# Summing Strassen-Winograd products in one PSUM bank, and moving three modulations into the mixers' input products

## The chip, the cores and the metric

The kernel runs on one core of one Trainium2 chip. The metric is device time in microseconds (us) for one launch. The engines are named as in the profile: PE is TensorE (its weight loads are PEld), DVE is VectorE, ACT is ScalarE, POOL is GpSimd and SP is SyncE, which issues nearly all DMAs. PSUM has eight banks here: five under the name `ps`, two `pt`, one `po`, each of 128 x 512 fp32.

## The reference, cut to what matters

One diffusion-transformer layer on 1024 latent tokens and 256 context tokens, of width 1024, all fp32:

```
ml = split(silu(c) @ w_mod + b_mod, 9)              # nine modulations; mc likewise from c_ctx
x  = x + 0.5 * ml[2] * swiglu(modulate(rms_norm(x, norm1_g), ml[0], ml[1]), ffn1_w_in, ffn1_w_out)
...                                                  # cx likewise, with mc
hx = modulate(rms_norm(x, norm2_g), ml[3], ml[4])
bg, cg, vc, q, k, v, gt = split(hx @ w_in, ...)      # the input products of the mixers
y_conv = bg * short_conv(cg * vc, conv_w)
...                                                  # attention over context and latent keys: o
x  = x + ml[5] * (sigmoid(gt_c) * (y_conv @ w_branch_conv) + sigmoid(gt_a) * (o @ w_branch_attn)) @ w_out
x  = x + 0.5 * ml[8] * swiglu(modulate(rms_norm(x, norm3_g), ml[6], ml[7]), ffn2_w_in, ffn2_w_out)
return rms_norm(x, final_g)
# swiglu(h, w_in, w_out): a, b = split(h @ w_in, 2); (silu(a) * b) @ w_out
```

## The kernel before, in words

Activations lie transposed: channels on partitions, tokens along the free axis, in two chunks of 512 latent tokens, C0 and C1, and the context chunk CC. Each fp32 matmul is made of three: both operands are split into a high part (a cast by ACT) and the rest (a subtraction by DVE), and high*high, high*low and low*high are added in PSUM.

Three large products, the inputs of the two feed-forwards and those of the mixers, take their weights in *pairs of columns*: two blocks of 128 output channels (for a feed-forward, one of the half `a` and one of the half `b`). A pair's 2 x 2 blocks of weights times the 2 x 2 blocks of the activation (channel halves by token chunks) are computed by the Strassen-Winograd scheme with seven products instead of eight. Class `Winograd` holds it. Its seven right operands `r1` to `r7` are made once per stage; `lefts` makes the left operands pair by pair: two loads into `raw` (three buffers), three sums `s1`, `s2`, `s3` on POOL and a fourth that overwrites `s2`, and a split of each operand into a buffer `wl` (four buffers; ACT casts, then DVE subtracts). `product(i)` is one product: twelve matmuls of 512 columns into a fresh `ps` bank. There are 22 pairs in each feed-forward and 20 in the mixers.

The seven products of a pair are added up on DVE, each add reading one bank of PSUM: `first` copies product 1 to `u` (ACT) and adds 2 for `c`; `second` adds 6 to `u`, then 7 for `v`, and subtracts 4 from `v` for `b`; `third` adds 5 to `v` and to `u`, and 3 to `u`. The results are (c, b) for C0 and (u, v) for C1. `spill` takes silu(c) * b and writes it to DRAM (`hd`); in the mixers, conv and gates take their place.

In the first pairs of each stage (`ahead`: 13 in the first feed-forward, 9 in the mixers, 9 in the second) products 1 and 2, which need only C0's norm, run ahead of the others while C1's norm is made (`start`, `start_by_half`). Their `u` and `c` go to DRAM (`ucd`), all but the first two, and `fetch` brings them back one pair early. So an ahead pair has five products in the loop, in the order 6, 7, 4, 5, 3, and a later pair has seven, 1, 2, 6, 7, 4, 5, 3.

`later_mod(m)` computes a modulation: per half of 512 columns eight steps, each a load `rawm` and a multiply-add into `macc` on DVE, four empty steps, a split, six empty steps, two matmuls with `ones_r` and a DMA that turns the row into columns (`mcol`): 19 steps a half. Modulations 0 to 4 run in the first feed-forward. Modulation 5 (`mix_steps`, 8 steps in each round `i` of the mixers with `i > 2`), 6 and 7 (`late_steps`, while the branches are merged and `w_out` is applied) and 8 (`last_steps`, in the second feed-forward) come later. A round `i` of the mixers is two pairs, or three where `i` is odd.

From pair 14 on (`SIDE_FROM`) the first feed-forward also runs the context tokens with each pair's split weights (`side`), and after pair 13 it catches up on the first 14.

No order is written out by hand in these stages: a scheduler lists the instructions of each engine by a timeline of its own, and each engine then runs its list strictly in that order, waiting on semaphores. SP's DMA queue is such a list too.

Of the kernel before, what the change touches and what calls it, by code (L numbers as in the profile page):

```python
# [20 lines left out]
KD = D // P  # L21
# [19 lines left out]
SIDE_FROM = 14  # L41
# [10 lines left out]
def tile_dit_layer(  # L52
# [434 lines left out]
    class Winograd:  # L487
# [6 lines left out]
        def __init__(self, xs, gain, mod, m, pairs, plain=False, ahead=3, side_from=None):  # L494
# [10 lines left out]
            self.n_ahead, self.side, self.started, self.n_left = ahead, None, [], 0  # L505
# [46 lines left out]
        def norm1(self, turned=None):  # L552
# [23 lines left out]
            for k in range(4):  # L576
# [11 lines left out]
                dve.tensor_sub(out=t2, in0=t2, in1=f[:, 1])  # L588
# [24 lines left out]
        def lefts(self, pairs, side_from):  # L613
# [29 lines left out]
            for j, (wa, wb) in enumerate(pairs):  # L643
                side = side_from is not None and j >= side_from
                a, b = cols(wa), cols(wb)
# [4 lines left out]
                if j >= n:  # L650
                    yield from map(parts, a)
                yield parts(s2)
                yield parts(s3)
                if side:
                    yield parts(b[0])
                yield parts(b[1])
                yield parts(s1)
                pool.tensor_sub(out=s2, in0=a[1], in1=s2)
                yield parts(s2)
                if side_from is not None and j == side_from - 1:  # L660
                    for wa, wb in pairs[:side_from]:
                        yield from map(parts, cols(wa) + cols(wb))

# [12 lines left out]
        def terms(self, ps, w, i, k):  # L676
# [3 lines left out]
            matmul(ps, wh, r[:, 1], start=False, stop=False)  # L680
            matmul(ps, wl, r[:, 0], start=False, stop=k == 3)

        def product(self, i):
            w, ps = self.left(), ps_s()
            for k in range(4):
                self.terms(ps, w, i, k)
            if self.side:
                self.side(i, w)
            return ps

        def first(self):

            u, c = ttile("u"), ttile("c")
            act.copy(out=u, in_=self.product(1))
            dve.tensor_add(out=c, in0=u, in1=self.product(2))
            return u, c
# [61 lines left out]
        def next_first(self):  # L758
            if not self.started:
                return self.first()  # L760
            self.fetch()
            uc = self.started.pop(0)
            self.fetch()
            return uc

        def second(self, u):
# [1093 lines left out]
```

## Time and profile before

| | |
|---|---|
| three runs | 2680.39, 2682.8, 2686.76 us; median 2682.8 |
| the profiled execution | 2685.79 us, of which the span of the profile is 2684.0 |
| PE busy | 2639.7 us, 98% of the span |
| DVE busy | 2006.2 us, 75% |
| ACT busy | 1171.3 us, 44% |
| POOL busy | 557.9 us, 21% |
| DMA | 376.93 MB, mean 140 GB/s |
| mean granted PE clock | 0.995 |

The stages by their place in the span, read off the tiles in the trace: start and first norm to about 131 us, ahead pairs of the first feed-forward to about 309, pair 13 and the context's catching up to about 450, its later pairs to about 690, its output product to about 900; the mixers' start to about 950, their pairs to about 1290; keys, queries and attention to about 1835; merging and `w_out` to about 2021; the second feed-forward's start to about 2072, its pairs to about 2447, its output and the last norm to the end.

A PE that is busy is not necessarily at its peak: the ends of matmuls are modelled, so the number of matmuls in a stretch says as much as the busy time. The tables by stretches give, per engine, busy us and in brackets the number of instructions, then the granted clock as a share of full speed, the DMA engines' share and GB/s.

### The profile page before, as it was taken

The numbers are of one execution on the slowest core, as the hardware profiler recorded it, in microseconds if no ns is written. First come the engines' busy times: TensorE is split into PE (matmuls) and PEld (weight loads), VectorE is DVE, ScalarE is ACT, GpSimd is POOL, SyncE is SP. The second block draws the span as 40 slices with busy tenths as digits, with TensorE's granted clock in tenths as the row PEclk, the third lists the DMA queues.
The fourth block names the chain that finished last, engine by engine and source line by source line (L and its number), as shares of the span: only waits on it lengthen the run. The fifth ranks groups of instructions, "written<-read, shape, count | busy, mean of one in ns | idle before, by whom it ended". The sixth has DMA issues, their size and how long they took to land.

```text
span 2684.0 us, 36956 instructions
## 1 busy us (share of the span) xinstructions
PE 2639.7 (98%) x13373; PEld 2221.6 (83%) x13373; DVE 2006.2 (75%) x3356; ACT 1171.3 (44%) x2317; POOL 557.9 (21%) x449
## 2 busy tenths in 40 slices
PE   8999999999999999999999999999999999999998
PEld 5787899888778878888999888887888788888888
DVE  5788966888877899877387676675668876667885
ACT  6533454433444633333245566673236233334453
POOL 0134201211010044333032112141001442330200
PEclk9999999999999999999999999999999999999999
DMA  8565465345974345242312532113734543228741
GB/s 317 194 204 177 144 221 173 109 130 209 288 182 122 111 158 180 95 130 75 103 48 91 87 87 64 32 44 110 262 100 144 181 154 95 86 88 288 182 90 64
DMA packets 370000, 376.93 MB, mean 140 GB/s; under 512 B 19590, under 2 KB 258328, under 8 KB 369816
## 3 DMA queue, kind: packets, MB, share of 16 engines
q1 hardware_dynamic: 359000, 353.03, 40.8%
q0 software_dynamic: 10816, 21.53, 4.9%
q8 instruction: 105, 1.72, 0.3%
q14 instruction: 79, 0.65, 0.1%
HBM read 306.78 MB, written 67.67 MB: 140 GB/s over the span
## 4 chain that ended last, share of the span: by engine, by line
PE 84%; DVE 4%; DMA 2%; issue 2%; POOL 1%; ACT 1%; SPq 0%; DVEq 0%; POOLq 0%; ACTq 0%
PE ps L90 69%; PE pt L90 7%; PE po L90 7%; DVE wl L90 1%; DMA raw<-in_ffn_w_in_dram 1%; DMA ws<-in_ffn_w_out_dram 1%; DVE r L90 1%; DMA rawm<-in_w_mod_dram 1%; POOL s L90 0%; DVE macc L90 0%; POOL ol L90 0%; DVE u L90 0%; DVE uc L90 0%; DVE nt L90 0%; DVE v L90 0%
## 5 line engine op out<-in xcount | busy, mean ns | idle before, releaser
L90 PE MATMUL ps<-r,wl 128*128 128x512 f32 x5196 | 1204.7, 391 | 12.2 <-DVE wl L90 5.3
L90 PEld LDWEIGHTS ps<-r,wl 128*128 128x128 f32 x5196 | 971.6, 188 | 221.9 <-DVE wl L90 7.9
L90 ACT CAST wl<-s 128x512 fp32r<-128x512 f32 x254 | 156.7, 619 | 322.6 <-PE ps L90 219.3
L90 POOL TENSOR_TENSOR s<-raw 128x512 f32<-128x512 f32 x64 | 93.4, 1459 | 891.2 <-DMA raw<-in_ffn_w_in_dram 380.9
L90 ACT CAST wl<-raw 128x512 fp32r<-128x512 f32 x287 | 177.5, 619 | 219.6 <-PE ps L90 157.3
L90 DVE TENSOR_TENSOR wl<-raw,wl 128x512 fp32r<-128x512 f32 x287 | 201.9, 705 | 62.1 <-ACT wl L90 59.6
L90 DVE TENSOR_TENSOR wl<-s,wl 128x512 fp32r<-128x512 f32 x254 | 229.8, 905 | 21.3 <-ACT wl L90 19.7
L90 POOL TENSOR_TENSOR s<-raw,s 128x512 f32<-128x512 f32 x64 | 103.9, 1624 | 362.3 <-DVE wl L90 362.3
L90 DVE SCALAR_TENSOR_TENSOR macc<-rawm,silu_c,macc 128x512 f32<-128x512 f32 x178 | 149.8, 858 | 31.7 <-DMA rawm<-in_w_mod_dram 30.7
L90 PE MATMUL ps<-wh,r 128*128 128x256 f32 x768 | 141.6, 285 | 0.0
L90 DVE TENSOR_TENSOR u<-u,ps 128x512 f32<-128x512 f32 x174 | 118.0, 678 | 28.7 <-PE ps L90 28.5
L90 DVE TENSOR_TENSOR pts<-pt,pts 128x512 fp32r<-128x512 f32 x160 | 108.7, 685 | 35.7 <-ACT pts L90 33.5
L90 ACT CAST pts<-pt 128x512 fp32r<-128x512 f32 x160 | 93.3, 595 | 94.8 <-PE pt L90 90.9
L90 DVE TENSOR_REDUCE m<-ps 128x1 f32<-128x512 f32 (+1 forms) x192 | 109.9, 594 | 23.3 <-PE ps L90 22.3
L90 ACT CAST rh<-hid 128x512 fp32r<-128x512 f32 x132 | 80.9, 620 | 101.6 <-PE ps L90 89.3
L90 PE MATMUL ps<-rh,wl 128*128 128x512 f32 x360 | 122.3, 390 | 2.8 <-ACT rh L90 2.8
L90 PEld LDWEIGHTS ps<-wh,r 128*128 128x128 f32 x768 | 120.6, 192 | 0.0
L90 PE MATMUL po<-pts,vh 128*128 128x512 f32 x256 | 111.4, 440 | 0.2 <-ACT pts L90 0.2
L90 PE MATMUL ps<-wl,r 128*128 128x256 f32 x384 | 108.8, 283 | 0.0
L90 ACT CAST wh<-raw 128x512 fp32r<-128x512 f32 (+1 forms) x85 | 67.9, 801 | 88.8 <-PE ps L90 57.8
L90 DVE TENSOR_TENSOR rl<-hid,rh 128x512 fp32r<-128x512 f32 x132 | 89.8, 684 | 20.2 <-PE ps L90 9.8
L90 PE MATMUL ps<-kl,qs 128*128 128x512 f32 x384 | 104.3, 395 | 0.0
(314 smaller groups left out, 5118.6 us busy)
## 6 DMA issues: line engine op xcount, KB each, us to landing
raw<-in_ffn_w_in_dram SPq DMA_DIRECT2D x130, 512.0 KB
raw<-in_ffn_w_out_dram SPq DMA_DIRECT2D x72, 512.0 KB
rawm<-in_w_mod_dram SPq DMA_DIRECT2D x136, 256.0 KB
raw<-in_w_in_dram SPq DMA_DIRECT2D x61, 512.0 KB
hid<-hd SPq DMA_DIRECT2D x40, 512.0 KB
ws<-in_ffn_w_out_dram POOLq DMA_DIRECT2D x30, 512.0 KB, 6.6
ucd<-uc SPq DMA_DIRECT2D x25, 512.0 KB
hd<-c SPq DMA_DIRECT2D x40, 256.0 KB
```

The lines of the kernel that those rows point to most:

```text
L90: inst = getattr(self.engine, name)(*args, **kw)
```

## The change

The sums move from DVE into PSUM. Product 1 keeps its bank, called `x` here: 6 is added onto it, then 7, then the *negative* of 4 (its right operand is made with the sign turned, in `norm1`). Product 5 has a second bank, `z`, and 3 is added onto it. Between two products in the bank `x` ACT copies the partial sum out: after 1 (`u`, and `c` = `u` + product 2, as before), after 6 (`u6`) and after 7 (`v`). DVE adds `z` to `v` after product 5 and to `u6` after product 3; the results are (c, x) and (u6, v), where x is read from PSUM. For an ahead pair, ACT first copies the fetched `u` into the bank `x`. A pair's products are written in the order 6, 5, 7, then the next pair's head (its 6 if it is ahead, else its 1 and 2), then 4 and 3, then the next pair's 6 if it is not ahead; `order` gives the left operands in that order, and `fetch` loads a pair's weights when product 7 of the pair before asks for its operand.

Modulations 5, 6 and 7 all run in the mixers: 9 + 8 steps in each round from `i = 1`. None is left for merging and `w_out`. In the mixers a gate is written into a tile of its own.

```
@@ norm1
-                dve.tensor_sub(out=t2, in0=t2, in1=f[:, 1])
+                dve.tensor_sub(out=t2, in0=f[:, 1], in1=t2)
                 self.keep(4, k, t2)
@@ lefts
+            def fetch(j):
+                ...
+                a, b = map(cols, pairs[j])
+                s1, s2, s3 = ttile("s1"), ttile("s2"), ttile("s3")
+                pool.tensor_add(out=s1, in0=b[0], in1=b[1])
+                pool.tensor_sub(out=s2, in0=s1, in1=a[0])
+                pool.tensor_sub(out=s3, in0=a[0], in1=b[0])
+                state[j] = {0: b[0], 1: a[0], 2: a[1], 3: s2, 4: b[1], 5: s1, 6: s2, 7: s3}
+            for j, i in self.order(side_from):
+                ...
+                fetch(j)
+                yield parts(state[j][i])
+                if i == 6:
+                    pool.tensor_sub(out=state[j][3], in0=state[j][2], in1=state[j][3])
+                if i == 7 and j + 1 != side_from:
+                    fetch(j + 1)
@@ terms, product
-            matmul(ps, wh, r[:, 0], start=k == 0, stop=False)
+            matmul(ps, wh, r[:, 0], start=k == 0 and not on, stop=False, on=on)
...
-        def product(self, i):
-            w, ps = self.left(), ps_s()
+        def product(self, i, onto=None, j=None):
+            w, ps = self.left(), ps_s() if onto is None else onto
...
@@ first, second, third give way to
+        def head(self, j):
+            ...
+            if j < self.n_ahead:
+                self.fetch()
+                u, c = self.started.pop(0)
+                x = ps_s()
+                act.copy(out=x, in_=u)
+                self.fetch()
+                return x, self.with_sixth(x), c
+            u, c = ttile("u"), ttile("c")
+            x = self.product(1, j=j)
+            act.copy(out=u, in_=x)
+            dve.tensor_add(out=c, in0=u, in1=self.product(2, j=j))
+            return x, None, c
+        def with_sixth(self, x):
+            u = ttile("u6")
+            act.copy(out=u, in_=self.product(6, x))
+            return u
+        def results(self, apart=None):
+            opened = self.tail(self.head(0))
+            for j in range(self.n_pairs):
+                x, u, c = opened
+                z, v = self.product(5), ttile("v")
+                act.copy(out=v, in_=self.product(7, x))
+                dve.tensor_add(out=v, in0=v, in1=z)
+                ...
+                if j + 1 != apart:
+                    opened = self.head(j + 1)
+                self.product(4, x, j)
+                yield c, x
+                self.product(3, z)
+                dve.tensor_add(out=u, in0=u, in1=z)
+                if j + 1 != apart:
+                    opened = self.tail(opened)
+                yield u, v
+                ...
@@ modulations
-    mix_steps, late_steps, last_steps = later_mod(5), (step for m in (6, 7) for step in later_mod(m)), later_mod(8)
+    mix_steps, last_steps = (step for m in (5, 6, 7) for step in later_mod(m)), later_mod(8)
@@ mixers
-        if i > 2:
-            run(mix_steps, 8)
+        if i:
+            run(mix_steps, 9)
...
+        if i:
+            run(mix_steps, 8)
@@ merging, w_out
-                run(late_steps, 4)
...
-            if ch == C0:
-                run(late_steps, 4)
```

The lists of both programs hold the same number of matmuls on PE (13286). DVE's list has 256 instructions fewer, ACT's 159 more. Three places show how the lists change. In the rows, `ps`, `r` and `wl` carry a tile's running number, `r6` is the right operand of product 6, and `x3` at the end of a row stands for three matmuls in a row.

PE before, the mixers' first pair: products 6, 7, 4 and 5 each have a bank of their own.

```order
L90 MATMUL ps_1603_8818<-r6_1548_8592,wl_1584_8748 128x512 x3
L90 MATMUL ps_1603_8818<-r6_1563_8653,wl_1584_8748 128x512
L90 MATMUL ps_1605_8836<-r7_1512_8452,wl_1588_8768 128x512 x2
L90 MATMUL ps_1612_8863<-r4_1515_8462,wl_1590_8785 128x512 x2
L90 MATMUL ps_1603_8818<-r6_1563_8653,wl_1584_8748 128x512 x2
L90 MATMUL ps_1614_8880<-r5_1513_8455,wl_1602_8815 128x512 x2
```

PE after, the same place: the bank `ps_1525` is the bank `x` of this pair and `ps_1534` its bank `z`.

```order
L90 MATMUL ps_1525_8708<-r6_1488_8547,wl_1509_8642 128x512
L90 MATMUL ps_1534_8741<-r5_1487_8544,wl_1513_8663 128x512 x2
L90 MATMUL ps_1525_8708<-r6_1488_8547,wl_1509_8642 128x512 x2
L90 MATMUL ps_1525_8708<-r7_1437_8346,wl_1515_8680 128x512 x3
L90 MATMUL ps_1525_8708<-r7_1454_8413,wl_1515_8680 128x512 x3
L90 MATMUL ps_1525_8708<-r7_1471_8480,wl_1515_8680 128x512 x3
L90 MATMUL ps_1525_8708<-r7_1486_8541,wl_1515_8680 128x512 x3
L90 MATMUL ps_1537_8772<-r6_1439_8352,wl_1532_8721 128x512 x3
```

Product 7 now follows product 6 in the same bank with nothing between them, so that ACT's copy of `u6` lies between the two; the next pair's product 6 has moved up behind 7.

DVE before, the mixers' round `i = 3`, between the splits of products 2 (`wl_1797`) and 6 (`wl_1799`) of its last pair: `macc0` is a modulation's sum, `y` the short convolution.

```order
L90 TENSOR_TENSOR wl_1797_9847<-raw_1790_9820,wl_1797_9847 128x512
L90 SCALAR_TENSOR_TENSOR macc0_1775_9758<-rawm_1781_9774,silu_c_93,macc0_1775_9758 128x512
L90 TENSOR_TENSOR b_1785_9784<-v_1784_9783,ps_1796_9833 128x512
L90 SCALAR_TENSOR_TENSOR macc0_1775_9758<-rawm_1782_9777,silu_c_93,macc0_1775_9758 128x512
L90 TENSOR_SCALAR y_1801_9884<-u_1753_9642,cols_84 128x512
L90 TENSOR_TENSOR v_1784_9783<-v_1784_9783,ps_1798_9850 128x512
L90 TENSOR_TENSOR u_1754_9643<-u_1754_9643,ps_1798_9850 128x512
L90 TENSOR_TENSOR wl_1799_9865<-s2_1793_9825,wl_1799_9865 128x512
```

DVE after, the same round, from two rows behind the split of its first pair's product 7 to the split of the next pair's product 6 (`wl_1696`).

```order
L90 SCALAR_TENSOR_TENSOR macc0_1671_9472<-rawm_1674_9479,silu_c_93,macc0_1671_9472 128x512
L90 TENSOR_TENSOR v_1681_9511<-v_1681_9511,ps_1680_9498 128x512
L90 SCALAR_TENSOR_TENSOR macc0_1671_9472<-rawm_1675_9482,silu_c_93,macc0_1671_9472 128x512
L90 SCALAR_TENSOR_TENSOR macc0_1671_9472<-rawm_1676_9485,silu_c_93,macc0_1671_9472 128x512
L90 SCALAR_TENSOR_TENSOR macc0_1671_9472<-rawm_1677_9488,silu_c_93,macc0_1671_9472 128x512
L90 SCALAR_TENSOR_TENSOR macc0_1671_9472<-rawm_1678_9491,silu_c_93,macc0_1671_9472 128x512
L90 TENSOR_SCALAR y_1690_9570<-u_1649_9354,cols_84 128x512
L90 SCALAR_TENSOR_TENSOR y_1690_9570<-u_1649_9354,cols_84,y_1690_9570 128x511
L90 SCALAR_TENSOR_TENSOR y_1690_9570<-u_1649_9354,cols_84,y_1690_9570 128x512
L90 TENSOR_TENSOR u6_1657_9396<-u6_1657_9396,ps_1680_9498 128x512
L90 TENSOR_TENSOR y_1690_9570<-y_1690_9570,c_1635_9281 128x512
L90 TENSOR_TENSOR wl_1696_9586<-s2_1694_9581,wl_1696_9586 128x512
```

Modulations now run while ahead pairs do; here six of their multiply-adds (one stands above the first row) and a convolution stand between two splits.

ACT before, ahead pairs of the first feed-forward: besides the casts, the silu of a fetched `c` and of `u`.

```order
L90 ACTIVATE u_334_1614<-u_334_1614 128x512
L90 CAST wl_389_1884<-s2_366_1773 128x512
L90 CAST wl_396_1911<-s2_394_1906 128x512
L90 ACTIVATE c_384_1861<-c_384_1861 128x512
L90 CAST wl_398_1931<-s3_395_1907 128x512
L90 CAST wl_400_1949<-raw_392_1903 128x512
```

ACT after, the same stage: `u_340` and `c_341` come from DRAM.

```order
L90 COPY v_337_1653<-ps_321_1560 128x512
L90 CAST wl_343_1678<-s1_329_1605 128x512
L90 CAST wl_344_1694<-s3_331_1607 128x512
L90 COPY u6_342_1677<-ps_339_1671 128x512
L90 COPY ps_357_1780<-u_340_1673 128x512
L90 ACTIVATE c_341_1674<-c_341_1674 128x512
L90 CAST wl_350_1722<-s2_348_1717 128x512
```

Three copies a pair have come into ACT's list, two of them out of a bank onto which PE's next product is to be added, one into the bank of the pair after it.

More of the change, by code (lines that the diff above doesn't have):

```diff
@@ L756, in fetch @@
                 self.started[0] = u, c
[L758 to L766, printed above, removed]
-            v, b = ttile("v"), ttile("b")
-            dve.tensor_add(out=u, in0=u, in1=self.product(6))
-            dve.tensor_add(out=v, in0=u, in1=self.product(7))
-            if self.side:
-                self.side(0, self.left())
-            dve.tensor_sub(out=b, in0=v, in1=self.product(4))
-            return v, b
```

120 lines of the change are left out of this document (71 added, 49 removed).

## The prediction

> **What bounds the kernel now.** I read the page's first part, then the span by stretches, then what PE waits for, then the rows behind the two or three places that the change can touch.
>
> ```profile
> span 2684.0 us, 36956 instructions
> PE 2639.7 (98%) x13373; PEld 2221.6 (83%) x13373; DVE 2006.2 (75%) x3356; ACT 1171.3 (44%) x2317; POOL 557.9 (21%) x449
> ```
>
> PE is busy 98%: 44.3 us of the span are all that waits on PE can give back, wherever they lie. The table by stretches says where (us of PE, DVE and so on, with their instructions in brackets).
>
> ```profile
> 131.00:220.00 89.00, 88.42 (x391) 72.37 (x389) 74.65 (x100) 27.38 (x46) 35.94 (x24) 1.00 0.60 189
> 220.00:309.00 89.00, 84.51 (x360) 66.96 (x360) 74.68 (x114) 29.46 (x55) 36.95 (x25) 0.98 0.51 160
> 450.00:690.00 240.00, 240.00 (x1245) 203.80 (x1244) 187.84 (x294) 92.09 (x159) 42.40 (x29) 1.00 0.48 160
> 977.00:1087.00 110.00, 109.57 (x485) 90.07 (x484) 102.12 (x146) 34.04 (x58) 48.95 (x32) 1.00 0.50 161
> 1087.00:1290.00 203.00, 203.00 (x896) 167.55 (x895) 156.43 (x230) 70.35 (x117) 59.75 (x40) 1.00 0.34 108
> 1836.00:2021.00 185.00, 184.29 (x825) 151.00 (x824) 116.83 (x173) 63.14 (x88) 1.46 (x1) 1.00 0.52 167
> 2095.00:2195.00 100.00, 100.00 (x443) 82.55 (x442) 78.93 (x106) 31.19 (x52) 45.74 (x31) 1.00 0.60 180
> 2195.00:2447.00 252.00, 252.00 (x1114) 208.40 (x1113) 163.95 (x229) 84.52 (x140) 70.02 (x49) 1.00 0.34 110
> ```
>
> The row 2095:2195 is pure products: 443 matmuls in 100 us, 0.2257 us each, 2.71 us for a product of twelve. The mixers' pairs (485 in 110 us, where that pace gives 487; then 896 in 203) and the second feed-forward's (1114 in 252) already run at it, though DVE is busy 93% in 977:1087. There an emptier DVE wins nothing. Only the ahead pairs of the first feed-forward (131 to 309) fall short: 751 matmuls, where the pace gives 178 / 0.2257 = 789. That is 38 x 0.2257 = 8.6 us lost, with DVE busy 149.3 of 178. What PE waits for there:
>
> ```profile
> PE ps L90 <- ACT wl L90: 2.5, 4, 1.0
> PE pt L90 <- DVE sq_acc L90: 1.4, 1, 1.4
> PE ps L90 <- DVE wl L90: 1.2, 2, 0.6
> ```
>
> Split weights come late (`wl`), and once the context norm's sum. The chain that ended last shows how they get late (start, length, what):
>
> ```profile
> 195.65 5.58 DMA rawm<-in_w_mod_dram
> 201.31 1.67 DVE macc L90
> ...
> 210.54 5.88 DMA raw<-in_ffn_w_in_dram
> 216.59 1.42 POOL s L90
> 218.09 1.30 POOL s L90
> 220.07 1.55 DVE wl L90
> ```
>
> A modulation's load holds DVE, DVE's late result holds a write in SP's list, the next weights are issued behind it, and PE is short of a split at 220.
>
> **The change part by part.** *The sums.* No matmul goes or comes. Per pair four DVE adds go and ACT gains three copies (ahead pair) or two.
>
> ```profile
> L90 DVE TENSOR_TENSOR u<-u,ps 128x512 f32<-128x512 f32 x174 | 118.0, 678 | 28.7 <-PE ps L90 28.5
> L90 ACT COPY u<-ps 128x512 f32<-128x512 f32 x11 | 6.5, 587 | 12.3 <-PE ps L90 12.3
> ```
>
> That is 64 pairs x 4 x 0.678 = 174 us off DVE, and (31 x 3 + 33 x 2) x 0.587 = 93 us onto ACT, 44% busy before. Both lie beside PE, so the direct gain is nil. The indirect one is in 131:309: 13 pairs x 2.7 = 35 us less on DVE, 64% in place of 84%. Of the 8.6 us, the wait on `sq_acc` and the slow clock behind it (1.4 and 1.6, below) stay, because the chain from the context's modulation column to that norm is not shortened. Of the other 5.6 I take half, **-2.8 us**, since part of that chain is DMA and POOL time, which stays. Its ends: all of it, -5.6; or +4, about as much again as the late splits cost now, as SP's list now issues a pair's two loads back to back behind the previous `hd` write, where one of them used to go a pair earlier.
>
> *New waits in the bank.* Product 7 may not write bank `x` before ACT has copied `u6` out of it, nor 4 before `v` is out. In most pairs a whole product stands between (2.71 us). In four places hardly anything does: 6 to 7 in the first pair of the mixers (the first PE place shown above) and of the second feed-forward, 7 to 4 in the last pair of that, and 7 to 4 in one mixers pair with two matmuls between. The trace has no such wait on a large bank; nearest is a modulation's row, PE to ACT's copy to PE:
>
> ```profile
> 26.49 0.39 PE L90 MATMUL ps<-accl,ones_r 128*1 128x512 f32 x1
> 26.92 0.58 ACT L90 COPY mrow<-ps 1x512 f32<-1x512 f32 x1 [2.69 <-PE ps L90]
> 27.55 0.40 PE L90 MATMUL pt<-ident,mrow 1*128 1x1 f32 x4 [0.67 <-ACT mrow L90]
> ...
> 61.60 0.40 PE L90 MATMUL pt<-ident,mrow 1*128 1x1 f32 x4 [0.74 <-ACT mrow L90]
> ```
>
> From the start of the last matmul (26.49) to the next (27.55) are 1.06 us, 0.83 more than the pace. Three places at 0.83 and one at 0.4 make **+2.9 us**. Least 1.2 (at the two stage starts PE waits for the last right operands anyway), most 4 (a cast of 0.62 ahead of a copy in two places).
>
> Where a product does stand between, 2.71 - 0.83 leaves 1.9 us for what is ahead of the copy in ACT's list; a cast is 0.62, so three fit. I put that at nothing. If that cover goes, each late copy is paid at once, since PE's list has the product next.
>
> *Modulations 6 and 7 into the mixers.* What they leave, 1836:2021, has PE at 184.29 of 185: **0** to win, at most 0.7. What they enter is busier. Rounds 1 to 3 (977:1087, eight pairs) get 3 x 17 = 51 steps, 8 in 19 of which load: 21.5 loads and multiply-adds, where about 8 ran. The rows of 1000:1100 price them:
>
> ```profile
> L90 DVE TENSOR_TENSOR wl<-s,wl 128x512 fp32r<-128x512 f32 x27 | 24.7, 914 | 1.0 <-ACT wl L90 0.9
> L90 DVE SCALAR_TENSOR_TENSOR macc<-rawm,silu_c,macc 128x512 f32<-128x512 f32 x7 | 7.4, 1051 | 0.2
> L90 DVE SCALAR_TENSOR_TENSOR y<-u,cols,y 128x512 f32<-128x512 f32 x6 | 6.4, 1086 | 0.0
> L90 DVE TENSOR_SCALAR y<-u,cols 128x512 f32<-128x512 f32 x6 | 5.5, 947 | 0.0
> L90 DVE SCALAR_TENSOR_TENSOR y<-u,cols,y 128x511 f32<-128x511 f32 x6 | 5.5, 910 | 0.0
> ```
>
> DVE there: 102.1 - 8 x 2.7 + 13.5 x 1.05 = 94.7, and loads that come late, of which the first feed-forward has the price:
>
> ```profile
> DVE macc L90 <- DMA rawm<-in_w_mod_dram: 7.6, 5, 2.6
> ```
>
> (131:309, 24 loads: 0.32 each.) 21.5 x 0.32 makes 6.9, together 101.6 of 110, as full as before. So the mean load decides nothing; lumps do. In the DVE rows shown for round 3, from behind the split of product 7 to the next pair's 6, stand six multiply-adds at 1.051, a convolution (0.947 + 0.910 + 1.086 + 0.68), two adds (1.35) and the split (0.914): 12.2 us; with the cast and split before them (0.62 + 0.75) 13.6. Four buffers `wl` hold four products, 10.85 us. So PE could stand 2.7 us there; as DVE may be ahead, I take half, with a little for the other rounds: **+1.6 us**, between 0 and 8 (that lump once in each of rounds 1 to 3). The moved loads, 32 x 256 KB, pass SP's list between weight loads; DMA is busy 0.50 there against 0.60 in 131:220, where PE lost 0.6 us in 89.
>
> *Turned sign, gates into own tiles, earlier `gain3`:* same instructions in other places, 0.
>
> Sum: -2.8 + 2.9 + 0 + 1.6 = **+1.7 us**. The profiled execution took 2685.8 us, 1.8 of it outside the span; so 2687.5 for that execution. The three runs have their median 3.0 us lower, so I give **2684.5 us** for a median run. A measurement of this kernel can tell about 0.2%, 5.4 us, from no change.
>
> *The clock.* Each short wait could also slow PE's clock (stretches with PE's busy time, granted clock, DMA):
>
> ```profile
> 291.58:294.99 3.41, 2.06 (x12) 1.00 0.01 4
> 294.99:298.41 3.42, 3.42 (x10) 0.50 0.27 98
> 740.00:743.40 3.40, 0.56 (x3) 1.00 0.99 380
> ```
>
> Behind a stretch in which PE had been busy 2.06 of 3.41 us came one at half clock, 10 matmuls in place of 15: 1.1 us by their number, 1.7 by half the stretch, and I take 1.6. But at 740, busy only 0.56 of 3.40, none came. So 1.35 us of waiting can cost 1.6 more, and need not; a wait of 0.83 is shorter. I put it at nothing and keep it as a rival. The Trainium skill, "TensorE: Matmul & The Clock Gate", Part 1, has the clock halve after at least one idle window of about 3.4 us; by that rule no wait of this change would slow the clock, and the first of these rows does not agree with it.
>
> **The rivals.**
>
> *Slower: DVE's lumps in the mixers.* Place: the six runs of modulation steps (9 and 8) in rounds 1 to 3. If, besides the one lump counted, the others also get past 10.85 us between two splits, PE stands at each. For: DVE is at 93% there already, and a load has kept it waiting up to 3.8 us (below). Against: the other long lumps in the new list come to 6.8, 6.7 and 6.5 us by the same rows, so it decides only if loads wait some 4 us each. Price: five of six at 2.7, 13.5 in place of 1.6: 2682.8 - 2.8 + 2.9 + 13.5 = **2696.4**.
>
> ```profile
> DVE macc L90 <- DMA rawm<-in_w_mod_dram: 42.5, 29, 3.8
> ACT c L90 <- DMA c<-ucd: 53.6, 13, 8.5
> ```
>
> The second row adds to it: ACT waits for a fetched `c`, and behind that wait now stand the copies. From the copy of `u6` to the next pair's cast PE has four products, 10.85 us, less 2.8 for a copy, the silu, cast and split: 8.0 us, just under the longest wait, 8.5.
>
> *Slower: the clock.* All four new waits are followed by a half-clock stretch: 4 x 1.6 = 6.4, **2690.9**. For: the row at 291. Against: the row at 740, and waits that are shorter than 1.35.
>
> *Faster.* The lighter DVE clears 131:309 wholly, with the wait on `sq_acc` (1.4) and its slow clock (1.6), the new waits at the stage starts vanish behind those for right operands (1.2 left), and the mixers lose nothing: -5.6 - 3.0 + 1.2 = -7.4, **2675.4**. For: DVE falls to 64% there. Against: DMA and POOL links of the chain stay.
>
> **How the numbers follow.** Forecast 2684.5 with 50%; lumps 20%, clock 11%, faster 19%. The ends of the terms add up to -5.1 (-5.6 + 1.2 - 0.7) and +16 (4 + 4 + 8), which seldom meet. The range reaches to the faster rival and past the lumps: **2675 to 2698**. Chances: faster by over 0.2% (below 2677.4) 0.19, within 0.50, slower (above 2688.2) 0.31.
>
> **What would show it.** Right: some 760 to 780 matmuls in the first feed-forward's ahead pairs for the same work, so that they end 2 to 4 us earlier; new waits of PE on ACT's `u6` and `v`, 0.7 us each, a handful; 443 matmuls in 100 us in later pairs; no change from merging to `w_out`. Wrong: PE waiting on `v` or `u6` in most pairs (the 1.9 us of cover are not there), a row of PE on DVE `wl` of more than 5 us in the mixers, or PE on DVE `v` or ACT `ps` (a bank filled too late), each times the number of pairs; or half-clock stretches that were not there.

## The result, and the profile after

| | before | after |
|---|---|---|
| median of four runs each | 2682.75 us | 2743.2 us (2741.3 to 2747.6) |
| ratio, with its 95% interval | | 1.0226 (1.0207 to 1.0245) |
| the profiled execution | 2685.8 us | 2741.4 us |
| mean granted PE clock | 0.995 | 0.989 |

The change costs 60.5 us. The forecast was 2684.5, from 2675 to 2698. The page of the kernel after:

```profile
span 2739.2 us, 36831 instructions
PE 2658.9 (97%) x13373; PEld 2226.6 (81%) x13373; DVE 1854.4 (68%) x3100; ACT 1250.9 (46%) x2476; POOL 545.8 (20%) x449
```

The work is near what the prediction said it would be: as many matmuls, DVE 152 us lighter (forecast 174), ACT 80 us heavier (forecast 93). Of the 55.2 us that the span grew, 36.0 are idle time of PE, which went from 44.3 to 80.3 us. The other 19.2 are busy time of PE for the same matmuls, at a lower granted clock. Where, the table by stretches of the kernel after shows (columns as above; the stretches are the ahead pairs of the first feed-forward, the mixers' pairs that are ahead and those that are not, and the same two of the second feed-forward):

```profile
131.00:317.00 186.00, 175.90 (x757) 141.93 (x756) 109.85 (x163) 76.50 (x136) 61.48 (x45) 0.98 0.51 165
955.00:1225.00 270.00, 244.39 (x1008) 192.54 (x1007) 188.66 (x271) 99.43 (x180) 90.70 (x59) 0.96 0.43 139
1225.00:1335.00 110.00, 109.84 (x483) 89.39 (x482) 80.01 (x108) 44.35 (x77) 32.10 (x21) 1.00 0.40 128
2130.00:2250.00 120.00, 112.54 (x488) 90.52 (x487) 66.67 (x86) 46.21 (x83) 44.45 (x33) 1.00 0.49 156
2250.00:2500.00 250.00, 249.32 (x1100) 205.87 (x1099) 136.14 (x172) 96.16 (x166) 72.36 (x49) 1.00 0.37 120
```

The later pairs, which fetch no `u` and `c` and run beside few modulation steps, go at nearly full pace in the new order of products (483 matmuls in 110 us, 1100 in 250, where the pace of 0.2257 us gives 487 and 1108). The ahead pairs do not: 955:1225 has 1008 matmuls where it gives 1196. DVE is busy 70% there and ACT 37%, so neither is full. What PE waits for in the whole run, the largest rows:

```profile
PE ps L90 <- DVE wl L90: 22.2, 14, 5.0
PE ps L90 <- ACT v L90: 10.9, 9, 3.3
PE ps L90 <- ACT wl L90: 6.6, 7, 3.1
PE pt L90 <- ACT acch L90: 6.3, 1, 6.3
...
PE ps L90 <- DVE v L90: 3.0, 3, 1.3
```

The kernel before has no row for ACT's `v` or `acch`, and the first row is there

```profile
PE ps L90 <- DVE wl L90: 5.3, 5, 2.8
```

So 16.9 of the 36.0 us are splits that DVE makes too late.

One wait, in round 2 of the mixers, in full (the timeline of 1019 to 1037; start, length, engine, what, and idle time before it with its releaser):

```profile
1018.73 12.40 PE L90 MATMUL ps<-r,wl 128*128 128x512 f32 x54
...
1020.17 7.21 SPq L90 DMA_DIRECT2D rawm<-in_w_mod_dram  x2
...
1023.32 0.59 ACT L90 COPY ps<-u 128x512 f32<-128x512 f32 x1 [4.43 <-DMA u<-ucd]
...
1029.83 0.75 DVE L90 SCALAR_TENSOR_TENSOR macc<-rawm,silu_c,macc 128x512 f32<-128x512 f32 x1 [1.12 <-DMA rawm<-in_w_mod_dram]
...
1030.61 5.84 SPq L90 DMA_DIRECT2D rawm<-in_w_mod_dram  x6
1031.11 0.68 DVE L90 TENSOR_TENSOR wl<-s,wl 128x512 fp32r<-128x512 f32 x1
1034.75 0.75 DVE L90 SCALAR_TENSOR_TENSOR macc<-rawm,silu_c,macc 128x512 f32<-128x512 f32 x1 [2.96 <-DMA rawm<-in_w_mod_dram]
1035.42 0.68 DVE L90 TENSOR_TENSOR wl<-s,wl 128x512 fp32r<-128x512 f32 x1
1036.02 1.53 DVE L90 SCALAR_TENSOR_TENSOR macc<-rawm,silu_c,macc 128x512 f32<-128x512 f32 x2
...
1036.16 2.07 PE L90 MATMUL ps<-r,wl 128*128 128x512 f32 x4 [5.03 <-DVE wl L90]
1036.80 0.59 ACT L90 COPY v<-ps 128x512 f32<-128x512 f32 x1 [8.18 <-DVE macc L90]
```

Read from the bottom. ACT stands 8.18 us at a copy of `v`, and what releases it is a multiply-add on DVE, the first of the two at 1036.02: the tile that `v` gets still holds a modulation's load, and comes free when that has been read. The multiply-add ahead of these waits 2.96 us for its load, and in DVE's list the split that PE needs next stands behind it (1035.42), so PE, done with its last product at 1031.13, stands 5.03 us. The loads go out late, in bursts that stretch over 7.21 and 5.84 us on SP, and ACT's copy of the next `u` into its bank waits 4.43 us for a load too. The first feed-forward's ahead pairs show the same: of the 8.4 us for which PE waits there for DVE's splits, 5.9 are two waits at splits that stand behind a multiply-add that waits for its load. One of them:

```profile
223.54 0.75 DVE L90 SCALAR_TENSOR_TENSOR macc<-rawm,silu_c,macc 128x512 f32<-128x512 f32 x1 [2.21 <-DMA rawm<-in_w_mod_dram]
224.21 0.68 DVE L90 TENSOR_TENSOR wl<-s,wl 128x512 fp32r<-128x512 f32 x1
224.32 0.59 ACT L90 COPY v<-ps 128x512 f32<-128x512 f32 x1 [3.53 <-DVE macc L90]
...
224.94 1.51 PE L90 MATMUL ps<-r,wl 128*128 128x512 f32 x5 [3.37 <-DVE wl L90]
```

`rawm`, `macc`, `u`, `c`, `u6`, `v`, the three sums, `y` and the gates all come from one pool of eleven small tiles (128 x 512) that nothing in my prediction counted.

### The profile page after: what moved, and what is told of

Same layout as the page of the kernel before. It is cut to its first block, busy times and chain, and to the rows that moved or that the text cites. A ratio compares the mean times of both kernels' runs of the same rounds, so it can differ in the third digit from the quotient of the medians.

```text
span 2739.2 us, 36831 instructions
## 1 busy us (share of the span) xinstructions
PE 2658.9 (97%) x13373; PEld 2226.6 (81%) x13373; DVE 1854.4 (68%) x3100; ACT 1250.9 (46%) x2476; POOL 545.8 (20%) x449
## 5 line engine op out<-in xcount | busy, mean ns | idle before, releaser
L90 PE MATMUL ps<-r,wl 128*128 128x512 f32 x5196 | 1225.8, 394 | 47.1 <-DVE wl L90 21.9
L90 DVE TENSOR_TENSOR wl<-s,wl 128x512 fp32r<-128x512 f32 x254 | 204.8, 809 | 128.2 <-ACT wl L90 126.7
L90 DVE TENSOR_TENSOR wl<-raw,wl 128x512 fp32r<-128x512 f32 x287 | 228.3, 797 | 64.8 <-ACT wl L90 63.5
L90 POOL TENSOR_TENSOR s<-raw,s 128x512 f32<-128x512 f32 x64 | 94.2, 1471 | 411.0 <-DVE wl L90 410.4
L90 DVE SCALAR_TENSOR_TENSOR macc<-rawm,silu_c,macc 128x512 f32<-128x512 f32 x178 | 134.3, 776 | 59.4 <-DMA rawm<-in_w_mod_dram 58.3
L90 ACT COPY v<-ps 128x512 f32<-128x512 f32 x64 | 37.5, 586 | 156.1 <-PE ps L90 88.8
L90 DVE TENSOR_TENSOR rl<-hid,rh 128x512 fp32r<-128x512 f32 x132 | 89.7, 684 | 23.1 <-PE ps L90 11.9
```

What stands on the lines that cost most here:

```text
L90: inst = getattr(self.engine, name)(*args, **kw)
```

## The experiments

The theory, called *buffers*: the eleven small tiles run out in ahead pairs, so copies out of bank `x` and modulation loads wait for a tile, and on ACT, DVE and SP, which run their lists in order, the next splits and loads stand behind them. The rivals: *modulations* (DVE and DMA too full in the mixers) and *bank* (the new order of products and PE to ACT to PE itself).

All runs in one table. Both kernels run 13,373 matmuls; the last five columns compare the start of the n-th one with that in before's profile, in us lost (+) or won (-) up to n = 3250 (near the end of the first feed-forward's pairs), 4500 (the mixers' start), 6000 (the end of the mixers' pairs), 10500 (the second feed-forward's start) and the end. Where modulations 6 and 7 are moved forward, their eight matmuls carry about 1.4 us from the fourth of these columns to the third. The five kernels (after, e1, e7, e9, e18) whose lists are the same up to the mixers lose 7.9 to 13.5 in the first column: one stage of one profile is good to some 5 us.

| run | what | median us | ratio to before (95%) | ffn1 pairs | their end, output | mixers | attention, w_out | ffn2 |
|---|---|---|---|---|---|---|---|---|
| after | | 2743.2 | 1.0226 (1.0207-1.0245) | 7.9 | 7.8 | 37.8 | -6.5 | 8.2 |
| e1 | after, modulations back | 2724.1 | 1.0145 (1.0130-1.0160) | 10.6 | 6.6 | 10.2 | -0.2 | 9.9 |
| e2 | before, modulations moved | 2692.1 | 1.0024 (1.0014-1.0033) | 2.4 | -1.2 | 14.2 | -7.6 | 0.0 |
| e3 | after, 13 small tiles, 3 `wh` | 2725.9 | 1.0153 (1.0136-1.0170) | 9.9 | 1.6 | 22.6 | 0.0 | 2.6 |
| e4 | after, 11 small tiles, 3 `wh` | 2748.6 | 1.0233 (1.0215-1.0252) | 12.8 | 4.8 | 40.6 | -4.1 | 10.6 |
| e5 | after, `u`,`c` in `wh` | 2720.5 | 1.0143 (1.0120-1.0166) | 1.7 | 7.6 | 28.9 | -7.0 | 3.7 |
| e6 | after, 12 steps | 2739.9 | 1.0211 (1.0194-1.0228) | 12.4 | 3.6 | 36.8 | -8.2 | 8.8 |
| e7 | after, modulations in later rounds | 2744.3 | 1.0225 (1.0209-1.0240) | 11.9 | 8.1 | 38.1 | -5.9 | 8.0 |
| e8 | e5, `u` added by DVE | 2745.5 | 1.0230 (1.0212-1.0248) | 18.6 | 4.6 | 34.8 | -5.8 | 12.7 |
| e9 | after, `rawm` in `wh`, one ahead | 2723.3 | 1.0147 (1.0132-1.0162) | 13.5 | 8.8 | 14.4 | -6.4 | 9.9 |
| e10 | e1 + e5 | 2700.8 | 1.0070 (1.0054-1.0087) | 1.9 | 7.5 | 5.0 | -2.2 | 2.8 |
| e11 | e5 + e6 + e9 | 2709.8 | 1.0095 (1.0080-1.0110) | 7.2 | 2.6 | 12.8 | -6.1 | 7.8 |
| e12 | e2 + `u`,`c` and `rawm` in `wh` | 2702.3 | 1.0065 (1.0050-1.0080) | 12.1 | 0.2 | 9.4 | -7.2 | 2.8 |
| e13 | before, 13 small tiles, 3 `wh` | 2690.9 | 1.0024 (1.0014-1.0033) | -1.4 | 1.8 | 6.9 | 1.1 | -1.7 |
| e14 | e10, 12 steps, late modulations later | 2693.7 | 1.0028 (1.0018-1.0039) | 3.5 | 0.5 | 4.6 | -7.3 | 3.7 |
| e15 | before, late modulations two merges later | 2677.9 | 0.9973 (0.9963-0.9984) | -0.7 | -1.7 | 0.2 | -8.1 | 0.0 |
| e16 | before, four merges later | 2676.7 | 0.9968 (0.9957-0.9979) | 0.3 | -2.0 | 0.6 | -7.9 | 0.0 |
| e17 | e5 with two loads | 2728.3 | 1.0163 (1.0146-1.0179) | 11.3 | 9.6 | 30.5 | -6.9 | 5.2 |
| e18 | e9 without the lead | 2720.8 | 1.0137 (1.0122-1.0152) | 9.2 | 7.0 | 14.6 | -6.4 | 10.6 |

**e1 and e2, each half of the change by itself.**

```
e1: after, with the old places of later_mod(5), (6), (7):
-        if i:
-            run(mix_steps, 9)      # and 8 more
+        if i > 2:
+            run(mix_steps, 8)
+                run(late_steps, 4) # behind each merge and in w_out
e2: before, with the same lines the other way round
```

> The new sums with modulations 5 to 7 where they stood before (5 in the mixers' rounds from i = 3, 6 and 7 in merging and w_out). Theory buffers (the eleven small tiles of one pool run out in ahead pairs, so that a copy out of bank x waits for one to come free): the modulations hold three to five of them, so the mixers' loss of 30 us falls to about 10, the first and second feed-forward keep their 18 and 10: about 2722 us. Theory modulations (DVE and loads too full in the mixers): the mixers' 30 go wholly, 2713. Theory bank (PE to ACT's copy to PE is itself too long with one product between): nothing changes, 2743.

> The kernel before, its sums on DVE, with modulations 5 to 7 in the mixers as in the kernel after. Theory buffers: the old sums hold fewer small tiles across pairs, so little is lost, 2685 to 2695 us. Theory modulations: the mixers lose what they lose after, 30 us, or more since DVE has 35 us more to do there: 2712 or above. Theory bank: no loss, 2683.

e1 took 2724.1, e2 2692.1. Against the 2685.4 that before had beside them the sums alone cost 39 us and the modulations alone 7. Together they cost 60.5, so some 15 us come only when both are there: they compete for something, which speaks for *buffers* and against *bank* (e1 would have stayed at 2743; it came to the 2722 that *buffers* gave). But *modulations* is not empty: in e2 the mixers lose 14.2 us, with DVE's old adds. What PE waits for in the mixers of e2 (950 to 1215):

```profile
PE ps L90 <- DVE wl L90: 6.7, 6, 2.8
PE ps L90 <- ACT wl L90: 3.2, 4, 1.5
PE ps L90 <- ACT u L90: 2.8, 1, 2.8
```

It is hidden in e2's total by a gain of 7.6 in the fourth column, of which below.

**e3 and e4, two more small tiles, and the control.**

```
-    tpool = ctx.enter_context(tc.tile_pool(name="tpool", bufs=11))
+    tpool = ctx.enter_context(tc.tile_pool(name="tpool", bufs=13))   # e3 only
+WH = 3                                                               # buffers wh, were 4
```

> The kernel after with 13 small tiles in place of 11; the room comes from the buffers wh, three in place of four. Theory buffers: of the 50 us lost in ahead pairs and at the first feed-forward's end at least half come back, 2700 to 2718 us. Theories modulations and bank: DVE's work and the order of products are as they were, 2740 to 2745.

> Control for the run with 13 small tiles: the kernel after with three buffers wh in place of four and still 11 small tiles. All theories: 2743 us, within 5; whatever it differs from that is the price of the buffer wh.

13 tiles against 11, with three `wh` in both: 22.7 us less by the medians. By the profiled executions it is 28.0, of which 18.0 are in the mixers and 8.0 in the second feed-forward. The rivals had expected no change; *buffers* had expected more, 2700 to 2718. The control by itself, e4, is level with the kernel after (1.0233 against 1.0226). In the first feed-forward's ahead pairs two tiles brought nothing that can be told from 5 us.

**e13, the same two tiles for the old sums.**

> The kernel before, old sums and old places of the modulations, with 13 small tiles and three wh. Theory buffers: the old sums hold fewer tiles, so two more bring little, 2680 to 2690 us, where the new sums won 23. Rival (more small tiles help any version): 2665 to 2672.

2690.9, 1 us above what was expected: no gain in any stage that could be told from 5 us, and 6.9 lost in the mixers, all of it at their first pairs. The old sums have no run with three `wh` and 11 tiles, so what the missing `wh` cost them is not shown, and a small gain may be hidden behind it. A gain such as the 22.7 of the new sums is not there: it is the new sums that run out of tiles.

**e5 and e17, the fetched `u` and `c` out of the small tiles.**

```
-                u, c = ttile("u"), ttile("c")
-                for i, t in enumerate((u, c)):
-                    load(t, self.started[0][:, i])
-                self.started[0] = u, c
+                t = wpool.tile([P, 2, 512], F32, tag="wh", name=uniq("uf"), bufs=W_BUFS)
+                load(t[:], self.started[0][:])             # e17: two loads, of t[:, 0] and t[:, 1]
+                self.started[0] = t[:, 0], t[:, 1]
```

> The kernel after, but the fetched u and c of an ahead pair go into one buffer wh (idle in these stages) with one DMA, so two to four of the eleven small tiles are free. Theory buffers: as much or more back than with 13 tiles (23 us), 2700 to 2718 us. Theory fetch (ACT's copy of the fetched u into bank x waits for the DMA, and v, u6 and the casts stand behind it in ACT's list): one DMA in place of two and no wait for a free tile, so that wait shrinks too, below 2710. Theory bank: 2743.

> The kernel after with the fetched u and c in one buffer wh, but still by two DMAs, one for each half. Theory buffers: as with one DMA, 2716 to 2726 us. Rival (it was the number of DMAs in SP's list): 2735 or more.

e5 brought 22.7 us, e17 14.9 by the medians (its profiled execution, 2735.3, is the longest of its four). Both fell 2 to 3 us short of what *buffers* gave. Both keep the free tiles. Whether the second load costs the difference the totals do not tell, since the intervals of the two overlap. The first column does, where e5 and e10, with one load, lose 1.7 and 1.9 and e17 11.3. What ACT waits for in the ahead pairs there (131 to 320), in after:

```profile
ACT u L90 <- DMA hd<-u: 10.5, 3, 4.4
ACT u L90 <- DVE macc L90: 8.9, 3, 5.2
ACT ps L90 <- DMA u<-ucd: 8.0, 5, 3.6
ACT v L90 <- DVE wl L90: 7.7, 2, 4.3
```

A copy that "waits for" a write to `hd`, for a multiply-add or for a split waits for its tile: those are the tile's last readers. In e17 these rows are gone, and what is left is a wait for a fetched tile (`uf`, with `u` and `c` in it), first what PE waits for, then ACT:

```profile
PE ps L90 <- ACT v L90: 10.5, 4, 5.5
...
ACT uf L90 <- DMA uf<-ucd: 30.0, 10, 4.8
```

In e5 the second row is 12.0 and the first 6.2. The instruction that waits is the silu of the fetched `c`, and in ACT's list the copy of `v` that PE needs stands right behind it (e17, the longest of these waits of PE):

```profile
225.16 0.63 ACT L90 ACTIVATE uf<-uf 128x512 f32<-128x512 f32 x1 [4.69 <-DMA uf<-ucd]
225.70 0.57 ACT L90 COPY v<-ps 128x512 f32<-128x512 f32 x1
...
226.32 1.22 PE L90 MATMUL ps<-r,wl 128*128 128x512 f32 x2 [5.46 <-ACT v L90]
```

So in the first feed-forward freed tiles alone did not help: once they are free, the silu of the fetched `c` waits for its load instead, and `v` is queued behind it. My expectation for e17 named one cause for the whole; there are two, in one list.

**e9 and e18, the modulations' loads out of the small tiles.**

```
-                raw = ttile("rawm")
-                load(out=raw, in_=w_mod[0, k * P : (k + 1) * P, o : o + 512])
+                    if k % 2 == 0:
+                        fetch_two(k + 2)          # e18: fetch_two(k); two rows into one buffer wh
+                    raw = two[k - k % 2][:, k % 2]
```

> The kernel after, with the loads of modulations 5 to 8 taken two rows at a time into buffers wh (idle there) and one load ahead of the multiply-adds that use them; everything else as after. Theory lists (DVE's list has a multiply-add that waits for its load ahead of the split weights that PE needs, and the load waits for a small tile and for gates in SP's list): the mixers' 38 us fall to 10 to 15, as with the modulations moved back, and the 8 us won at the end of attention stay: 2712 to 2722 us. Rival (DVE's work itself, 1.05 us a multiply-add, is too much beside the splits): 2738 to 2745.

> The kernel after with the modulation loads of 5 to 8 two rows at a time into wh, but each issued with the multiply-adds that use it, none ahead. Theory buffers (the tiles were what mattered): 2720 to 2728 us, as with the lead. Rival (the lead mattered, since DVE stands at a multiply-add until its load is there): 2735 or more.

The mixers' loss fell from 37.8 to 14.4 and 14.6, and the lead made no difference; e18 came out as expected, e9 1 us above its range. Both also halve the number of loads in SP's list, which no run here separates from the tiles. But e3 against e4, with as many loads as in after, brings 18.0 us back in the mixers by two more tiles, so most of it was the tiles. What DVE waits for in the mixers (950 to 1215), after and e18:

```profile
DVE macc L90 <- DMA rawm<-in_w_mod_dram: 12.9, 10, 3.0
```

```profile
DVE wl L90 <- ACT wl L90: 34.9, 17, 6.8
DVE v L90 <- ACT v L90: 11.9, 4, 4.3
DVE u L90 <- PE ps L90: 9.4, 8, 1.7
DVE y L90 <- ACT ps L90: 2.7, 1, 2.7
```

The ten waits for a modulation's load are gone, with as many multiply-adds in the same rounds: DVE's work itself was not too much.

**e7, the modulations in the later rounds.**

```
-        if i:
-            run(mix_steps, 9)
+        if i > 3:
+            run(mix_steps, 13)
```

> The kernel after with modulations 5 to 7 run only from the second half of the mixers' round 3 on, 13 steps at a time, where the pairs are no longer ahead and fetch nothing. If the modulations hurt only together with fetched pairs (buffers): the mixers lose 10 instead of 38 and the 8 us won at the end of attention stay: about 2715 us. If their loads and multiply-adds hurt in any pair: 2728 to 2743.

2744.3, so the first of the two did not come true and the second did, 1 us above its range. The first rounds improve, and the later ones lose as much (8 waits of DVE for `rawm`, 14.4 us, between 1225 and 1340). Fetched pairs are not needed for the shortage; 13 steps at a time do as well.

**e8, `u` added by DVE.**

```
-                act.copy(out=x, in_=u)
...
+                self.product(6, x, fresh=True)
+                dve.tensor_add(out=u6, in0=u, in1=x)
```

> As the run with u and c in wh, but in ahead pairs u is not copied into bank x: product 6 opens the bank, and DVE adds u to each partial sum as it reads it (u6, v and the final x), so ACT has three copies less and waits for no fetched u, while DVE has three adds more. Order of products and banks are as after. Theory fetch: whatever is left in ahead pairs falls by half or more against the run with u and c in wh, 10 us or more below it. Theory bank (the products' order and the wait on one bank): no difference to it, within 5 us. If DVE's load decides: slower than it by 5 to 15.

None of the three: it is 25 us slower than e5. ACT waits for no `u`, but `u` now stays in its buffer `wh` until product 4, which may hold up the next fetch, and DVE has the waiting adds in ACT's place. The run changes several things at once and decides little.

**e6, the left-over half.** At the end of the first feed-forward's pairs the kernel after has one wait that before does not have:

```profile
688.20 0.58 PE L90 MATMUL pt<-acch,ones_r 128*1 128x512 f32 x1 [6.28 <-ACT acch L90]
```

It is the last half of modulation 4, run after the loop by `run(steps)`; before has the same half there, but in its list products stand around it, and in after's only transposes stand behind it.

```
-STEPS = (0, 6, 6, 6, 6, 6, 6, 6, 6, 6, 6, 6, 6, 0, 11)
+STEPS = (0, 6, 6, 6, 6, 6, 6, 6, 6, 6, 6, 6, 6, 0, 12)
```

> The kernel after with 12 instead of 11 modulation steps behind each pair of the first feed-forward from pair 14 on, so that the last half of modulation 4 does not run over the end of the pairs. Theory left-over (of the 10.6 us lost at 3250 to 3500 matmuls most is the wait for that half's row with nothing queued behind it): 2732 to 2736 us. Rival (small tiles hold the chain up all along, so the wait only moves ahead): 2741 to 2745.

The second column fell from 7.8 to 3.6, the median by 3.4 only, to between the two ranges. Beside e10 the same edit in e14 takes it from 7.5 to 0.5. The place is shown, and 4 to 7 us of price; in e6's total it is near what the runs scatter.

**e10, e11, e12, several repairs together.**

> The new sums with the modulations back as before and the fetched u and c in wh: both pressures on the small tiles off at once. If the two effects just add up (modulations back 19, u and c in wh 23): 2701 us. Theory buffers: a little more than that, since what is left in the mixers (10 us) goes too: 2695 to 2702, of which 10 are the left-over run at the end of the first feed-forward's pairs. Theory bank (ahead pairs are slow by themselves in the new order): 2715 or more.

> The kernel after with the three repairs: u and c in wh, modulation loads in wh one ahead, 12 steps. If each takes away the loss that its own run showed (first feed-forward 7, its end 7, mixers 25, second feed-forward 7): 2690 to 2700 us. If wh's four buffers are now what runs out in ahead pairs, 2715 or more.

> The old sums with modulations 5 to 7 in the mixers, u and c in wh, modulation loads in wh one ahead. Theory lists: the mixers' 14 us that the modulations alone cost there vanish, the 8 us at the end of attention stay won, and the first feed-forward's ahead pairs may win some of their 5.6: 2672 to 2680 us, faster than the kernel before. Rival (DVE's work): 2690 or above.

e10 came out as the sum (2700.8). e11 lies between its two ranges: 2709.8, with 12.8 left in the mixers, so the repairs do not add up; it may be that four buffers `wh` for both uses are short again, which no run shows. e12 came to 2702.3, which was the range of the rival, DVE's work. No run tells whether that is the reason: for the old sums these buffers cost 12 in the first feed-forward and the mixers' loss only fell from 14.2 to 9.4.

**e14, e15, e16, where the 8 us at the end of attention come from.** Before has this at the end of attention (timeline, first DVE, then PE):

```profile
1819.43 1.42 DVE L90 SCALAR_TENSOR_TENSOR macc<-rawm,silu_c,macc 128x512 f32<-128x512 f32 x1 [3.19 <-DMA rawm<-in_w_mod_dram]
1820.78 0.68 DVE L90 TENSOR_TENSOR pts<-pt,pts 128x512 fp32r<-128x512 f32 x1
...
1821.51 1.11 PE L90 MATMUL pt<-ident,pl 128*128 128x128 f32 x4 [3.64 <-DVE pts L90]
```

The scheduler had put the first multiply-adds of modulation 6 among attention's last splits; one waits for its load, and the split that PE needs stands behind. The granted clock between 1820 and 1840 is 0.83. The change got rid of this by moving modulations 6 and 7 away. It can be had without that:

```
                 run(merge(j, ch))
-                run(late_steps, 4)
+                if j > 1:                    # e16: j > 2, 6 steps, and 5 in w_out
+                    run(late_steps, 5)
```

> The kernel before with the steps of modulations 6 and 7 beginning two merges later and nothing else. If the 8 us are the wait on a load in DVE's list ahead of attention's splits, with its slow clock: 2675 to 2679 us. Rival (the later steps run into the second feed-forward's start): 2683 or more.

> The same, beginning four merges later, with more steps at a time (6 and 5). If the wait alone decides: as the run before it, 2675 to 2679 us; if the modulations' last row now comes too late for the second feed-forward: slower than that by a few us.

> New sums, u and c in wh, 12 steps, modulations back, but those of 6 and 7 begin two merges later, so that no multiply-add stands in DVE's list ahead of attention's last splits. Against the run with modulations back and u and c in wh (2700.8): 7 less at the first feed-forward's end, 6 to 8 less at attention's end: 2685 to 2690 us, level with the kernel before and 6 to 12 above the old sums with the same late modulations. Rival (the new sums win something once their costs are gone): below 2680.

Both are faster than the kernel before, and than after: 2677.9 (0.9973, 0.9963 to 0.9984) and 2676.7 (0.9968, 0.9957 to 0.9979). What PE waits for between 1780 and 1845, before and e15:

```profile
PE pt L90 <- DVE pts L90: 4.5, 3, 3.6
```

```profile
PE pt L90 <- DVE pts L90: 0.2, 1, 0.2
```

e14, the new sums with every repair, is at 2693.7, somewhat above the 2685 to 2690 expected, and 15.8 us behind e15, which differs from it by the sums (with the gates' own tiles) and their repairs alone. So the sums in PSUM win nothing here even then. One place of what is left can be named, the mixers' first pairs (950 to 977 in before). By the starts of the same matmuls all fourteen kernels with the new sums lose 5.6 to 8.3 us there, e14 5.6. Those with the old sums lose up to 1.5, e15 0.4; only e13, with one `wh` less, loses 7.1. The longest wait of PE there in e14 is

```profile
971.59 3.63 PE L90 MATMUL ps<-r,wl 128*128 128x512 f32 x7 [4.12 <-ACT wl L90]
```

The split comes late because POOL's sum ahead of it waits for a load of weights. SP issued that load at 964.42, when the fourth sum of the pair before had set its buffer free; in before that was at 956.56. No modulation shows in this chain, and why the fourth sum ends so late is not shown.

## Why the prediction was wrong, point by point

- **No matmul changes, the sums are free of direct gain, later pairs at pace: right.** DVE lost 152 us and PE got nothing for it.
- **The new direct waits, 2.9 us in four places: right in price.** In the last pair of the second feed-forward product 4 waits for `v`, with nothing between:

```profile
2498.43 3.02 PE L90 MATMUL ps<-r,wl 128*128 128x512 f32 x12 [0.68 <-ACT v L90]
```

  With the time that the profile counts as the matmul's own this is 0.84 us over the pace, where I had 0.83. The Trainium skill, "Perfetto Trace Analysis", Optimizing Tensor Performance, Matmuls, wants independent groups of matmuls to rotate through PSUM banks so that one is emptied while the next is filled. It adds that an accumulation group has one bank by construction, and the products in bank `x` are such a group. This row shows the price where nothing overlaps the copy; at 0.84 in a few places it is the small part of the loss.
- **"I put that at nothing", the 1.9 us of cover for an ACT copy: the step that failed.** It counted ACT's own work ahead of the copy, and that indeed fits. It did not ask what the copy itself must wait for: a free one of eleven tiles, and, ahead of it in the list, a `u` or `c` on its way from DRAM. (The wait for `c` stood in the prediction, but only as a help to one rival.) The copies, casts and loads that stand behind such waits then make DVE's splits late too, and that is the larger part: PE's waits on DVE `wl` grew from 5.3 to 22.2 us, those on ACT `v` from none to 10.9. The prediction named both signs of error ("PE waiting on `v` or `u6`", though nine waits are not most pairs, and PE on DVE `wl` above 5 us in the mixers, where it is 13.3 in 950 to 1225). The sums alone cost 39 us; 22.7 of e4's loss went with two more tiles, 22.7 of after's with `u` and `c` out of the pool. e10 has 15.5 left, of which the left-over half and the mixers' first pairs are known.
- **The first feed-forward's ahead pairs, -2.8 us: wrong in sign.** The column for all pairs of that feed-forward loses 7.9 to 13.5, and 5.9 to 10.1 of it lies in the ahead pairs. DVE fell to 59% there, but the links that I had said stay in the chain (SP's list, loads, ACT) got longer. With the tiles freed, e5 and e10 are 1.0 and 0.7 us faster than before in these pairs, less than the spread of single profiles.
- **Modulations in the mixers, +1.6 between 0 and 8: mis-sized.** By themselves they cost 14.2 there. My rival "DVE's lumps in the mixers" had five lumps, 13.5 us, and the condition that loads wait some 4 us each; waits of up to 3.0 were enough (ten of them in after). I gave it 20%. With the new sums it is 37.8 less e1's 10.2, some 28 us; 23 of these went when the modulations' loads left the pool (e9, e18).
- **Merging and `w_out`, 0 to win: wrong by 8 us in the other direction.** I looked at 1836 to 2021, where the code has these steps. The scheduler had put the first of them ahead of 1836. e15 shows the 8 us.
- **The left-over half of modulation 4, 4 to 7 us: not in the prediction at all.** It was in the order of PE's list: four matmuls on `acch` and `accl` with only transposes behind.
- **The clock, at nothing: wrong in size.** The waits of 0.8 to 0.9 us slowed nothing, as assumed; longer ones that came did (0.96 in 955:1225). PE's busy time grew by 19.2 us for the same matmuls, and the mean granted clock fell from 0.995 to 0.989, which is an estimated 16 us of the span by itself. So about a third of the loss is slow clock behind the waits, where my rival had 6.4.

What stays open: why e14 is still 16 us behind e15 (some 4 us in each of the feed-forwards and in the mixers; in the mixers the place is known), and how e8's loss divides.

## What to carry to other kernels

A value that moves from one engine's sum into a copy needs a buffer, and an engine that runs its list in order passes on any wait for it to all that is queued behind; so count live tiles per pool, across the steps that overlap, before asking whether the engine has time. In a table of waits, a copy that waits for an unrelated reader (a split, a store, a multiply-add) is waiting for its buffer. And look for work that is to be moved where the scheduler has put it, not where the code has it: the one gain of this change lay there, and was to be had by moving the work a few steps.

## What the runs showed of the hardware

Whether a wait slows PE's clock does not follow from its length alone. Two stretches of the kernel after, each just behind a wait with no other in the 5 us before; PE had been idle 2.16 us ahead of the first and 2.49 ahead of the second:

```profile
206.30:209.70 3.40, 3.40 (x15) 2.81 (x16) 0.69 (x1) 0.98 (x2) 0.00 (x0) 1.00 1.02 359
270.70:274.10 3.40, 3.40 (x9) 2.68 (x10) 1.78 (x3) 1.02 (x2) 0.00 (x0) 0.53 0.78 293
```

The first runs 15 matmuls in 3.40 us, the second 9. The Trainium skill, "TensorE: Matmul & The Clock Gate", Part 1, has the clock halve after at least one idle window of about 3.4 us, and calls the window free-running. The second row does not agree with a full idle window: 2.49 us were enough. By the starts of the matmuls, such a drop followed each wait of the kernel after that was 2.5 us or more over the pace, and none of the three from 1.7 to 2.3 that stood alone.

The kernel before shows that this is no threshold. There PE had been idle 2.84 us ahead of this stretch, and the clock stayed:

```profile
743.20:746.60 3.40, 3.40 (x14) 2.55 (x15) 3.40 (x6) 3.40 (x6) 1.21 (x1) 1.00 0.92 255
```

And the half-clock stretch at 294.99 that the prediction shows had come behind 1.35 us. What else decides no run here shows.
